# Half of the low weight parts of the first SwiGLU half step: a negated cast and an adding transfer in place of a VectorE subtraction

## The chip, the cores and the metric

The kernel runs on one core of a Trainium2 chip. The metric is the device time of one execution in microseconds; lower is better. Before the change it was 1975.11 us (median of two runs, 1974.4 and 1975.81).

## The reference

One decoder layer on 256 tokens of width 2048, in float32: a SwiGLU half step, a mixer of dilated attention and gated linear attention, cross-attention into 256 memory tokens, and a second SwiGLU half step.

```python
def swiglu(h, w_gate, w_up, w_down):
    return (jax.nn.silu(h @ w_gate) * (h @ w_up)) @ w_down

x = x + 0.5 * swiglu(rms_norm(x, ffn1_norm), ffn1_w_gate, ffn1_w_up, ffn1_w_down)   # D_FF = 5632
x = x + hybrid_mixer(rms_norm(x, mix_norm), pos, w_in, ..., w_out)
x = x + cross_attention(rms_norm(x, xattn_norm), rms_norm(mem, mem_norm), ...)
x = x + 0.5 * swiglu(rms_norm(x, ffn2_norm), ffn2_w_gate, ffn2_w_up, ffn2_w_down)
```

The change concerns the first line of the four alone, and of it only how the weights are prepared.

## The kernel before

**Weights.** All weights are float32 in HBM, packed by the host so that a group of four k tiles (128 rows each) of a chunk of 512 columns is one contiguous megabyte, 8 KB for each of the 128 partitions. TensorE multiplies them as `float32r`, so each weight is split in two parts of that type: `wh`, the weight rounded by a cast on ScalarE (L125), and `wl`, the rest, by a subtraction on VectorE (L126). The tokens (`xT`, `hT`, `mT`) are split the same way into a high and a low part.

**One group.** `wgroup` loads a group into `raw` (L115, issued by SyncE, three buffers) and splits it in two halves of two k tiles each. A half's `wh` and `wl` are tiles of 128 x 1024 elements, 0.5 MB; `WB = 4` buffers each. `mm3` then multiplies one half: for both token tiles and both k tiles three products, tokens' high part by `wh` (L134) and by `wl` (L135), tokens' low part by `wh` (L136), all summed in a PSUM tile `acc`. So a half group is 12 products of 128x128 by 128x512, a group 24.

**Order.** `proj` walks over the groups of a chunk. The loads and the split of the weights stand in `tc.high_priority(WPRI)`, so that they are put ahead in the queues of their engines as far as buffers allow. Products that need other engines' results are put off with `later` by so many half groups.

**The first half step.** `ffn` does eleven chunks of gate and up (four groups each) and then four chunks of down (eleven groups each). The first chunk of gate is split in single k tiles as the tokens arrive (`fine`). `load_x` brings the tokens a second time for their norm; the norm's factor is a power on GpSimd (`rpow`, L214). The second half step uses the same function with other weights.

**GpSimd** has little to do in the first half step: the gains of the tokens' first chunks at the start (L180), the power at 50 us, and memsets for the mixer (L342 and the lines behind it) after it. Before the change GpSimd issues no transfers.

Of the kernel before, what the change touches and what calls it, by code (L numbers as in the profile page):

```python
# [17 lines left out]
S = 256  # L18
# [28 lines left out]
def layer_kernel(ctx: ExitStack, tc: tile.TileContext, A: dict, out: bass.AP):  # L47
# [22 lines left out]

    # products that wait for other engines are put off by so many half groups of a projection
    pend = []
# [13 lines left out]

# [1 line left out]
    gain = con.tile([P, 82], F32, name="gain")  # L88
    # the first loads in the order of their use; what is taken from xload and wload is already under way
    xload, wload = [], []  # L90
# [12 lines left out]

# [1 line left out]
    def wgroup(W, c, g, fine=None):  # L105
        """group g of chunk c of a packed weight, in halves; fine: per k tile, each after fine(k)"""
        n = W.shape[-1]
        kn = W.shape[-2]
        m = kn // 2
        with tc.high_priority(WPRI):  # L110
            if wload:
                raw = wload.pop(0)
            else:
                raw = wp.tile([P, kn, n], F32, tag="raw", name="raw")
                SY.dma_start(raw, W[c, g])  # L115
        for h in range(2):
            with tc.high_priority(WPRI):
                wh = wp.tile([P, m, n], F32R, tag="wh", name="wh", bufs=WB)
                wl = wp.tile([P, m, n], F32R, tag="wl", name="wl", bufs=WB)
                for i in range(m if fine else 1):  # L120
                    d = slice(i, i + 1) if fine else slice(0, m)
                    src = raw[:, m * h + d.start:m * h + d.stop]
                    if fine:
                        fine(m * h + i)
                    SC.copy(wh[:, d], src)  # L125
                    V.tensor_sub(wl[:, d], src, wh[:, d].bitcast(F32))  # L126
            yield [(kn * g + m * h + kk, wh[:, kk], wl[:, kk]) for kk in range(m)]

    def mm3(acc, lhs, half, first, last, ts=range(TT)):
        """adds lhs(k, t).T @ w for the k tiles of a half group"""  # L130
        for t in ts:
            for i, (k, wh, wl) in enumerate(half):
                lh, ll = lhs(k, t)
                PE.matmul(acc[t], lh, wh, start=first and i == 0, stop=False)  # L134
                PE.matmul(acc[t], lh, wl, start=False, stop=False)  # L135
                PE.matmul(acc[t], ll, wh, start=False, stop=last and i == len(half) - 1)  # L136

    def proj(W, c, lhs, groups, fine=None, last=False):
        """sum over the k tiles of the groups of lhs(k, t).T @ W[k, chunk c], for both token tiles"""
        n = W.shape[-1]  # L140
        acc = [pa.tile([P, n], F32, tag="acc", name="acc") for _ in range(TT)]
        groups = list(groups)
        for i, g in enumerate(groups):
            if fine and i:
                fine(4 * i)
            if last and i == len(groups) - 1:
                both = [w for half in wgroup(W, c, g) for w in half]
                for t in range(TT):
                    mm3(acc, lhs, both, i == 0, True, (t,))
                break  # L150
            for h, half in enumerate(wgroup(W, c, g, fine if i == 0 else None)):
                mm3(acc, lhs, half, i == 0 and h == 0, i == len(groups) - 1 and h == 1)
                tick()
        return acc
# [4 lines left out]

# [1 line left out]
    xT = {}  # L161
# [7 lines left out]
    def packed_load(src, k0, n):  # L169
        """n k tiles of a transposed chunk as the host packed it"""  # L170
        xr = U([P, n, S], F32, "xr")
        SY.dma_start(xr, src[k0 // 4, :, k0 % 4:k0 % 4 + n])
        return xr

    def packed(xr, k0, n, hi, lo, g0):
        """gain and split of what packed_load has brought"""
        if n == 1:
            SC.activation(xr[:, 0], xr[:, 0], AF.Copy, scale=gain[:, g0 + k0:g0 + k0 + 1])
        else:
            G.tensor_tensor(xr, xr, gain[:, g0 + k0:g0 + k0 + n].unsqueeze(2).broadcast_to([P, n, S]), op=ALU.mult)  # L180
        SC.copy(hi, xr)
        V.tensor_sub(lo, xr, hi.bitcast(F32))
# [6 lines left out]
    def norm_chunk(c, src, g0, ss):  # L189
        """src [tok, t, 512]: square sums into ss, gained and transposed halves into xT"""  # L190
        sumsq(c, src, ss)

        def turn():
            hi, lo = xtiles(c)
            for t in range(TT):
                tp = PM([P, 4, P], "tp")
                for j in range(4):
                    PE.transpose(tp[:, j], src[:, t, j * P:(j + 1) * P], ident)  # L198
                xg = W2([P, 4, P], "xg")
                V.tensor_tensor(xg, tp, gain[:, g0 + 4 * c:g0 + 4 * c + 4].unsqueeze(2).broadcast_to([P, 4, P]),  # L200
                                op=ALU.mult)
                sl = slice(t * P, (t + 1) * P)
                SC.copy(hi[:, :, sl], xg)
                V.tensor_sub(lo[:, :, sl], xg, hi[:, :, sl].bitcast(F32))

        later(1, turn)
# [20 lines left out]

# [1 line left out]
    def ffn(pre, r, after, fine=None, last=False):  # L229
        wg, wu, wd = (A[f"{pre}_w_{n}"] for n in ("gate", "up", "down"))  # L230
        hT = {}
# [11 lines left out]
        for f in range(NF):  # L243
            acc = proj(wg, f, lhs_x, range(4), fine if f == 0 else None)
            if callable(r):
                r = r()
            sg = []
            for t in range(TT):
                s = W2([P, 512], "sg")
                SC.activation(s, acc[t], AF.Silu, scale=r[:, t:t + 1])  # L250
                sg.append(s)
            acc = proj(wu, f, lhs_x, range(4))
            hs = []
# [9 lines left out]
        for c in range(NC):  # L263
            acc = proj(wd, c, lhs_h, range(NF), last=last and c == NC - 1)
            for t in range(TT):
                V.scalar_tensor_tensor(xs[c][:, t], acc[t], 0.5, xs[c][:, t], op0=ALU.mult, op1=ALU.add)
            after(c)

# [1 line left out]
    def head_scale(acc, r, r2, t, scale_in, sign, name):  # L270
        """per head of 128 columns: sign * r * (r^2 sumsq / 128 + eps)^-1/2, times 128^-1/2 if scale_in"""
        sq = W2([P, 4, HD], "sq")
# [17 lines left out]

# [1 line left out]
    mhalf = con.tile([P, P], F32, name="mhalf")  # L292
    V.memset(mhalf, -0.5)
    # the first function set, and the tensor engine's clock, while the first loads are under way
    warm = ST(1, "warm")
# [31 lines left out]

# [1 line left out]
    win = A["w_in"]  # L329
# [34 lines left out]

    # q, k of the gated heads
    def gated(which, c):
# [20 lines left out]

    # gate ranks, [rank, tok]: 16 columns of w_in, whose two parts are summed by the second product
    r2b = con.tile([P, TT, 32], F32, name="r2b")
# [12 lines left out]

    # log decays: 16 * log_a summed within chunks, [dk, head, tok]
    def decays():
# [30 lines left out]

    # decayed keys back to [tok, dk], the other chunk's rows zero
    kd = []
# [10 lines left out]

    # masked q k^T within chunks, transposed: [j, t, head, i]
    at = per_t("at")  # L450
# [64 lines left out]

    # output norm and gate
    mT = {}
# [26 lines left out]

# [1 line left out]
    # rope tables with the head norms' gains, q's negated  # L546
    gb = W2([P, 4, HD], "gb")
# [110 lines left out]

# [1 line left out]
    ssm = new_ss("ssm")  # L660
# [57 lines left out]

# [1 line left out]
    ss3 = new_ss("ss3")  # L720
# [7 lines left out]

# [1 line left out]
    acc = proj(A["xattn_w_q"], 0, lhs_x, range(4))  # L730
# [71 lines left out]

# [1 line left out]
    def store(c):  # L804
# [8 lines left out]
def _pack(w, n=512):  # L813
    """weights [K, N] as [N / n, groups, 128, k tiles, n]: each group of k tiles is one contiguous megabyte"""
    import numpy as np
# [7 lines left out]
def _columns(x):  # L823
    """tokens [S, D] as [chunks, 128, k tiles, S]"""
    import numpy as np

    return np.ascontiguousarray(np.asarray(x).T.reshape(NC, 4, P, S).transpose(0, 2, 1, 3))
# [26 lines left out]
def _constants():  # L854
    """What depends on the shapes alone: rope angles, which keys a query attends and how often."""
    import numpy as np
# [36 lines left out]
```

## Time and profile before

| | |
|---|---|
| profiled execution, span from the first to the last instruction | 1974.5 us |
| timed runs | 1974.4 and 1975.81 us, median 1975.11 us |
| granted TensorE clock, mean | 0.999 |
| TensorE busy | 1966.5 us |
| VectorE busy | 1039.2 us |
| ScalarE busy | 912.3 us |
| GpSimd busy | 61.2 us |
| read from HBM | 370.72 MB, 189 GB/s over the span |

The profile gives no time of its own for the profiled execution beside the span; the span lies within the timed runs. PE is TensorE's products, PEld its weight loads (they overlap), DVE VectorE, ACT ScalarE, POOL GpSimd, SP SyncE; a q behind a name is that engine's queue of instructions that are not counted as busy. L126 is line 126 of the kernel before. `out<-in` names the tiles an instruction writes and reads. DMA share is the mean busy share of the core's 16 DMA engines. In the timeline a row has the start and duration in us, and in brackets the idle time before it and what ended it.

### The profile page before, as it was taken

The page shows a single profiled execution, that of the slowest core. Times are in us where ns is not written, and L with a number is a line of the kernel's source. Part 1 is how long each engine was busy: PE and PEld are TensorE (multiplying, and loading weights), DVE is VectorE, ACT ScalarE, POOL GpSimd, SP SyncE. Part 2 cuts the span into 40 slices and gives each one's busy share as a digit, 9 for nine tenths or more (in the row PEclk, how much of TensorE's full clock was granted, in tenths as well). Part 3 has the DMA queues.
Part 4 walks back from the last instruction along what each step waited for, and adds up shares of the span by engine and source line. Part 5 has one row for each costly group of instructions (what it writes and reads, how often), then busy time and mean ns, then how long its engine had stood idle before and what let it go on. Part 6 is the DMA issues. An engine that isn't in the chain of part 4 may idle for free.

```text
span 1974.5 us, 22181 instructions
## 1 busy us (share of the span) xinstructions
PE 1966.5 (100%) x9000; PEld 1632.6 (83%) x9000; DVE 1039.2 (53%) x1102; ACT 912.3 (46%) x1115; POOL 61.2 (3%) x61
## 2 busy tenths in 40 slices
PE   9999999999999999999999999999999999999999
PEld 7888888888888888778888889888888888888887
DVE  6455444444455545546785566654444444444443
ACT  6444444444444436444576446544444444433332
POOL 2000000000000000002230000000000000000000
PEclk9999999999999999999999999999999999999999
DMA  8555555555555554445465554455555555555553
GB/s 308 187 191 189 192 192 192 187 188 187 189 190 190 195 204 149 171 156 201 172 219 204 196 186 154 173 192 192 188 187 188 188 189 190 191 192 202 203 204 116
DMA packets 57683, 374.26 MB, mean 190 GB/s; under 512 B 6475, under 2 KB 7627, under 8 KB 13932
## 3 DMA queue, kind: packets, MB, share of 16 engines
q1 hardware_dynamic: 56428, 370.74, 52.2%
q10 hardware_dynamic: 1152, 2.10, 0.3%
q8 instruction: 70, 1.15, 0.2%
q14 instruction: 33, 0.27, 0.0%
HBM read 370.72 MB, written 2.10 MB: 189 GB/s over the span
## 4 chain that ended last, share of the span: by engine, by line
PE 99%; DMA 0%; SPq 0%; DVE 0%; ACT 0%; POOL 0%; issue 0%; POOLq 0%
PE acc L136 32%; PE acc L134 32%; PE acc L135 32%; PE tp L239 1%; PE tp L198 1%; DMA xr<-in_xT_dram 0%; PE dsp L475 0%; PE op L492 0%; PE op L496 0%; PE tp L582 0%; PE sc L595 0%; PE op L629 0%; PE sc L738 0%; PE op L773 0%; PE tp L616 0%; PE zp L409 0%
## 5 line engine op out<-in xcount | busy, mean ns | idle before, releaser
L126 DVE TENSOR_TENSOR wl<-raw,wh 128x1024 fp32r<-128x1024 f32 (+1 forms) x690 | 845.6, 1227 | 855.5 <-ACT wh L125 855.1
L125 ACT CAST wh<-raw 128x1024 fp32r<-128x1024 f32 (+1 forms) x690 | 724.8, 1052 | 965.5 <-PE acc L136 944.6
L134 PE MATMUL acc<-wh,xTh 128*128 128x512 f32 x1824 | 714.8, 392 | 1.8 <-ACT wh L125 1.8
L135 PE MATMUL acc<-wl,xTh 128*128 128x512 f32 x1824 | 710.9, 390 | 1.0 <-DVE wl L126 1.0
L136 PE MATMUL acc<-wh,xTl 128*128 128x512 f32 x1824 | 710.7, 390 | 0.0
L134 PEld LDWEIGHTS acc<-wh,xTh 128*128 128x128 f32 x1824 | 342.5, 188 | 73.6 <-ACT wh L125 3.0
L135 PEld LDWEIGHTS acc<-wl,xTh 128*128 128x128 f32 x1824 | 343.0, 188 | 72.7 <-DVE wl L126 2.5
L136 PEld LDWEIGHTS acc<-wh,xTl 128*128 128x128 f32 x1824 | 342.8, 188 | 71.5
L134 PE MATMUL acc<-wh,hTh 128*128 128x512 f32 x704 | 274.3, 390 | 0.0
L136 PE MATMUL acc<-wh,hTl 128*128 128x512 f32 x704 | 273.9, 389 | 0.0
L135 PE MATMUL acc<-wl,hTh 128*128 128x512 f32 x704 | 273.9, 389 | 0.0
L136 PEld LDWEIGHTS acc<-wh,hTl 128*128 128x128 f32 x704 | 132.1, 188 | 27.5
L134 PEld LDWEIGHTS acc<-wh,hTh 128*128 128x128 f32 x704 | 132.1, 188 | 27.4
L135 PEld LDWEIGHTS acc<-wl,hTh 128*128 128x128 f32 x704 | 132.2, 188 | 27.2
L134 PE MATMUL acc<-wh,mTh 128*128 128x512 f32 x128 | 50.1, 392 | 0.0
L136 PE MATMUL acc<-wh,mTl 128*128 128x512 f32 x128 | 49.8, 389 | 0.0
L135 PE MATMUL acc<-wl,mTh 128*128 128x512 f32 x128 | 49.8, 389 | 0.0
L250 ACT ACTIVATE sg<-acc,r 128x512 f32<-128x512 f32 x44 | 30.1, 687 | 6.1 <-PE acc L136 6.1
L134 PE MATMUL acc<-wh,memh 128*128 128x256 f32 (+1 forms) x96 | 31.4, 327 | 0.0
L256 DVE SCALAR_TENSOR_TENSOR h<-acc,r,sg 128x512 f32<-128x512 f32 x44 | 30.9, 743 | 0.0
L136 PE MATMUL acc<-wh,meml 128*128 128x256 f32 (+1 forms) x96 | 30.6, 318 | 0.0
L135 PE MATMUL acc<-wl,memh 128*128 128x256 f32 (+1 forms) x96 | 30.5, 318 | 0.0
(249 smaller groups left out, 801.3 us busy)
## 6 DMA issues: line engine op xcount, KB each, us to landing
raw<-in_ffn_w_up_dram SPq DMA_DIRECT2D x88, 1024.0 KB, 4.8
raw<-in_ffn_w_down_dram SPq DMA_DIRECT2D x88, 1024.0 KB, 4.8
raw<-in_ffn_w_gate_dram SPq DMA_DIRECT2D x85, 1024.0 KB, 4.8
raw<-in_w_in_dram SPq DMA_DIRECT2D x48, 1024.0 KB, 4.8
raw<-in_w_out_dram SPq DMA_DIRECT2D x16, 1024.0 KB, 4.8
raw<-in_xattn_w_k_dram SPq DMA_DIRECT2D x4, 1024.0 KB, 4.7
raw<-in_xattn_w_q_dram SPq DMA_DIRECT2D x4, 1024.0 KB, 4.7
raw<-in_xattn_w_v_dram SPq DMA_DIRECT2D x4, 1024.0 KB, 4.9
```

Of the source, the lines that this page charges most:

```text
L125: SC.copy(wh[:, d], src)
L126: V.tensor_sub(wl[:, d], src, wh[:, d].bitcast(F32))
L134: PE.matmul(acc[t], lh, wh, start=first and i == 0, stop=False)
L135: PE.matmul(acc[t], lh, wl, start=False, stop=False)
L136: PE.matmul(acc[t], ll, wh, start=False, stop=last and i == len(half) - 1)
L198: PE.transpose(tp[:, j], src[:, t, j * P:(j + 1) * P], ident)
L239: PE.transpose(tp[:, j], hs[t][:, j * P:(j + 1) * P], ident)
L250: SC.activation(s, acc[t], AF.Silu, scale=r[:, t:t + 1])
L256: V.scalar_tensor_tensor(h, acc[t], r[:, t:t + 1], sg[t], op0=ALU.mult, op1=ALU.mult)
```

## The change

For the second half of each group in the first half step (all but the first chunk of gate), `wl` is no longer the difference `raw - wh` made by VectorE. ScalarE casts `raw` a second time with a scale of -1 into `wl`, and a transfer issued by GpSimd then adds the same weights, read again from HBM, onto `wl` in place. The first halves, the first chunk of gate and all other weights are split as before. The rest of the diff takes out comments and docstrings.

```diff
-    def wgroup(W, c, g, fine=None):
+    def wgroup(W, c, g, fine=None, dma=False):
...
         for h in range(2):
             with tc.high_priority(WPRI):
                 wh = wp.tile([P, m, n], F32R, tag="wh", name="wh", bufs=WB)
                 wl = wp.tile([P, m, n], F32R, tag="wl", name="wl", bufs=WB)
+                if dma and h == 1:
+                    SC.copy(wh, raw[:, m:])
+                    SC.activation(wl, raw[:, m:], AF.Copy, scale=-1.0)
+                    G.dma_start(wl, W[c, g][:, m:], accum_op=ALU.add)
+                    yield [(kn * g + m + kk, wh[:, kk], wl[:, kk]) for kk in range(m)]
+                    continue
                 for i in range(m if fine else 1):
...
-    def proj(W, c, lhs, groups, fine=None, last=False):
+    def proj(W, c, lhs, groups, fine=None, last=False, dma=False):
...
-            for h, half in enumerate(wgroup(W, c, g, fine if i == 0 else None)):
+            for h, half in enumerate(wgroup(W, c, g, fine if i == 0 else None, dma)):
...
     def ffn(pre, r, after, fine=None, last=False):
+        dma = pre == "ffn1"
...
-            acc = proj(wg, f, lhs_x, range(4), fine if f == 0 else None)
+            acc = proj(wg, f, lhs_x, range(4), fine if f == 0 else None, dma=dma and f > 0)
...
-            acc = proj(wu, f, lhs_x, range(4))
+            acc = proj(wu, f, lhs_x, range(4), dma=dma)
...
-            acc = proj(wd, c, lhs_h, range(NF), last=last and c == NC - 1)
+            acc = proj(wd, c, lhs_h, range(NF), last=last and c == NC - 1, dma=dma)
```

## The prediction

> **What bounds the kernel now.** I read the page's busy times and its chain first, to see which engine sets the end.
>
> ```profile
> PE 1966.5 (100%) x9000; PEld 1632.6 (83%) x9000; DVE 1039.2 (53%) x1102; ACT 912.3 (46%) x1115; POOL 61.2 (3%) x61
> ...
> PE 99%; DMA 0%; SPq 0%; DVE 0%; ACT 0%; POOL 0%; issue 0%; POOLq 0%
> ```
>
> TensorE is busy for all of the 1974.5 us span, and 99% of the chain lies on it. VectorE, which the change relieves, works half of the time. Whether TensorE ever waits for it is in the chain of waits:
>
> ```profile
> ACT wh L125 <- PE acc L136: 944.6, 603, 3.8
> DVE wl L126 <- ACT wh L125: 855.1, 617, 3.2
> ...
> PEld acc L134 <- ACT wh L125: 3.0, 4, 1.7
> ...
> PEld acc L135 <- DVE wl L126: 2.5, 4, 1.5
> ```
>
> The columns are total us, times and longest. The waits run the other way: ScalarE waits for TensorE to give a weight buffer back, VectorE waits for ScalarE. TensorE's waits for `wl` are 2.5 us in the whole kernel. So there is nothing to gain from a shorter VectorE queue. The question is only whether the new path brings `wl` in time. Two stretches, a settled one of the first half step and the start, show the transfers:
>
> ```profile
> core 0: us, PE busy (x) PEld busy (x) DVE busy (x) ACT busy (x) POOL busy (x), PEclk, DMA share, GB/s
> 10.00:20.00 10.00, 7.68 (x24) 5.30 (x24) 7.76 (x8) 6.10 (x10) 5.76 (x4) 0.83 1.03 407
> ...
> 200.00:400.00 200.00, 200.00 (x900) 165.97 (x899) 98.30 (x89) 86.35 (x91) 0.00 (x0) 1.00 0.53 191
> ```
>
> In the settled stretch TensorE has no idle time at the full clock and the DMA engines are 0.53 busy with 191 GB/s. At the start they are full: 407 GB/s is the most that they moved.
>
> **The budget of one half group.** A half group is two k tiles, twelve products. Its `wh` and `wl` each have four buffers. The timeline shows one turn:
>
> ```profile
> 299.71 0.39 PE L136 MATMUL acc<-wh,xTl 128*128 128x512 f32 x1
> 299.94 0.39 PE L134 MATMUL acc<-wh,xTh 128*128 128x512 f32 x1
> ...
> 300.14 1.05 ACT L125 CAST wh<-raw 128x1024 fp32r<-128x1024 f32 x1 [0.67 <-PE acc L136]
> ...
> 301.23 1.23 DVE L126 TENSOR_TENSOR wl<-raw,wh 128x1024 fp32r<-128x1024 f32 x1 [1.50 <-ACT wh L125]
> ...
> 302.48 11.21 SPq L115 DMA_DIRECT2D raw<-in_ffn_w_gate_dram  x3
> ...
> 302.66 0.39 PE L134 MATMUL acc<-wh,xTh 128*128 128x512 f32 x1
> 302.86 1.05 ACT L125 CAST wh<-raw 128x1024 fp32r<-128x1024 f32 x1 [1.08 <-PE acc L136]
> ...
> 308.10 0.39 PE L134 MATMUL acc<-wh,xTh 128*128 128x512 f32 x1
> ...
> 308.32 0.39 PE L135 MATMUL acc<-wl,xTh 128*128 128x512 f32 x1
> ...
> 313.74 1.05 ACT L125 CAST wh<-raw 128x1024 fp32r<-128x1024 f32 x1 [1.67 <-PE acc L136]
> ```
>
> Half groups start at 299.94 and 302.66, so one takes 2.72 us and a group 5.44 us. The half that ends at 300.10 frees the buffers; the cast into them starts at 300.14. Four buffers mean that they are used again three half groups later, in the half that starts at 308.10, where the first product with `wl` starts at 308.32. Today `wl` is ready at 301.23 + 1.23 = 302.46: 5.9 us to spare.
>
> **The change, part by part.** It concerns the second half of the groups of the first half step: 40 groups of gate (ten column chunks of four), 44 of up, 44 of down, so **128 half groups**.
>
> Removed: 128 subtractions of 1.23 us = 157 us of VectorE. They stand beside a busy TensorE, so they are worth 0. The most that relief of both engines could give is the waits quoted above, under 6 us.
>
> Added on ScalarE: 128 casts of 1.05 us = 135 us. In a settled group it then does 3 x 1.05 = 3.15 of 5.44 us; the 1.67 us of idle time ahead of the last cast shown covers it. But the cast lies on the new path: `wl` holds its negated value only at 300.14 + 2 x 1.05 = 302.24. From there to 308.32 the transfer has **6.1 us**, issue and landing included.
>
> Added on GpSimd: 128 issues, each waiting for the negated cast. Its queue is otherwise nearly empty in this stage:
>
> ```profile
> 49.99 0.72 POOL L214 TENSOR_TENSOR r<-r1m,mhalf 128x2 f32<-128x2 f32 x1 [24.43 <-DVE r1m L220]
> POOL glrT L342 <- PE acc L136: 637.5, 1, 637.5
> ```
>
> Behind a waiting transfer could stand only the one power at 50 us, which the first silu needs, and the memset after the half step. If a transfer stood behind that power instead, it could lose up to 24.4 us, once. I count 0 for it, since the code issues the power's inputs first and the transfers are raised by `WPRI`.
>
> Moved: `raw` was given back when VectorE had read it (302.46, and the load was issued at 302.48). Now it is given back by the negated cast at 302.24, the very moment when the adding transfer is released. **The 1 MB load and the adding transfer of 0.5 MB start together, every group.** The load itself is safe: what was asked for at 302.48 is first needed by the cast at 313.74, three groups on, over 11 us later, against 4.8 us to land (the next row).
>
> ```profile
> 18.39 0.33 SPq L115 DMA_DIRECT2D raw<-in_ffn_w_up_dram  x1
> 18.76 0.43 SPq L320 DMA_DIRECT2D x<-in_x_dram  x1
> ...
> raw<-in_ffn_w_up_dram SPq DMA_DIRECT2D x88, 1024.0 KB, 4.8
> ...
> raw<-in_ffn_w_gate_dram SPq DMA_DIRECT2D x4, 512.0 KB, 8.1
> x<-in_x_dram SPq DMA_DIRECT2D x4, 512.0 KB, 6.8
> ...
> graw<-in_w_rank_dram SPq DMA_DIRECT2D x1, 128.0 KB, 2.7
> ```
>
> The first two rows are issues in the timeline; the others give size and median us from issue to landing. No adding transfer and none issued by GpSimd is in this trace, so its duration D is bounded by these rows. Lower end: a plain 0.5 MB alone, between 2.7 us (128 KB) and 4.8 us (1 MB), on the line between them 3.6 us. Beside another load: `x` is 0.5 MB issued right behind 1 MB of `raw` (18.39 and 18.76), 6.8 us; half a megabyte of `raw` at the crowded start took 8.1 us. Upper end: the sum needs the old content of `wl` as well as the weights, so twice that, 13.6 us.
>
> I take a value nearest to the 1 MB row: two streams of 0.5 MB are read for it, so 4.8 us; the load that starts with it has 1.05 MB to move, which at 407 GB/s is 2.6 us, shared; and GpSimd's power above, on two columns, takes 0.72 us where an issue of SyncE takes 0.33, so I add 0.4 us, an estimate. **D = 7.8 us.** The `x` row with a second stream of 0.52 MB at 407 GB/s gives 6.8 + 1.3 = 8.1, near it.
>
> *The sum.* A `wl` buffer of a second half comes round every four half groups, 10.88 us. If D exceeds 6.1 us the turn is longer by the excess: 128 transfers over the two buffers are 64 turns, and TensorE waits 64 x (7.8 - 6.1) = **109 us**. As a check on bandwidth: the settled 0.53 is one megabyte per group; an adding half counted double makes 1.06 in 5.44 us. Against the 1.03 of the full stretch a group would be 5.60 us, 128 x 0.16 = 20 us, so the turn is the tighter limit, not the bytes. Nothing after the first half step changes. 1974.5 + 109 = **2083 us**. The span of 1974.5 lies inside the shown runs (1974.4 to 1975.81, median 1975.11), so no correction is made. The measurement can tell about 2%, 39.5 us, from no change; that is D = 6.7 us.
>
> The Trainium skill, Collectives: The Full Stack, section The bandwidth ceiling, says that a transfer which adds runs at half the rate of a copy, because it reads two sources through one ring. Nothing in this trace shows it; by that rule the sum would stay at 109 us; without it the plain price, weighed among the rivals, would hold.
>
> **Rivals.**
>
> *The transfer stays hidden* (not slower). If an adding transfer shares so well that it lands within 6.1 us of the cast, TensorE never waits: 1975 us. For it: an ordinary megabyte lands in 4.8 us, the DMA engines are idle almost half of the time. Against: it starts in the load's busiest moment, every time. It decides at D = 6.1 us; up to D = 6.7 us the time stays within 2%, and a transfer that costs no more than a plain one, 3.6 + 2.6 + 0.4 = 6.6 us, falls there too (64 x 0.5 = 32 us, 2007 us). Chance 0.32. The Trainium skill, DMA: Bandwidth & Descriptors, section Anatomy of one DMA, gives a GpSimd-issued transfer 2.0 us plus its bytes at 436 GB/s, an estimate of 3.2 us here, which would make this rival right; no run here shows one yet.
>
> *The transfer is much slower* than the bytes say: the add itself, or GpSimd's writing of 128 row transfers, costs several us each. At the upper end, D = 13.6 us, 64 x 7.5 = 480 us, 2455 us. TensorE would then stand still for several us at a time, and the 10-20 us row shows a granted clock of 0.83 where it was 7.68 of 10 us busy: a further loss. For it: nothing in the trace bounds the price of the add. Chance of D over 10.4 us: 0.16.
>
> *VectorE was the hidden limit* (faster). It would need products waiting for `wl`; the waits are under 6 us in all, 0.3%. Chance of over 2%: 0.01.
>
> **How the numbers follow.** The forecast, D between 6.7 and 10.4 us (2013 to 2250 us), has 0.51. Within 2% is 0.32, slower by over 2% 0.51 + 0.16 = 0.67, faster 0.01. The range takes in the hidden case and the forecast's whole, 1972 to 2250 us, and leaves out the slow tail.
>
> **What the profile would show.** If I am right: the memset behind the first half step, which runs at 49.99 + 0.72 + 637.5 = 688 us, comes near 795; before it TensorE's idle time ahead of the products with `wl` is released by DMA, about 1.7 us each second group or 0.85 each; the new transfers land in 7 to 9 us, the loads of `raw` in over 4.8; the DMA share there is about 0.8 to 0.9, and 128 x 0.52 = 67 MB more come from HBM; from the mixer on all is as before. If the transfer is hidden, the settled stretch has TensorE at 200 of 200 us with D under 6.1. What would make me wrong: a D far from 7.8, up or down, since every us of it is 64 us of time; or a TensorE clock below 1.00 in the waits.

## The result and the profile after

The changed kernel takes 2208.75 us (two runs, 2206.84 and 2210.66) against 1975.11 us: a ratio of 1.1184, 95% interval [1.1166, 1.1202]. It is slower, as forecast, and the time lies within the range of 1972 to 2250 us. But the forecast was 109 us more and the measured change is 234 us, over twice as much.

The page of the changed kernel, busy times, chain by engine, and transfers by queue (packets, MB, share of 16 engines' span):

```profile
PE 2033.0 (92%) x9000; PEld 1650.9 (75%) x9000; DVE 884.8 (40%) x974; ACT 1032.8 (47%) x1243; POOL 172.0 (8%) x189
...
q0 software_dynamic: 18432, 67.12, 18.9%
...
PE 67%; DMA 24%; issue 6%; ACT 2%; DVE 0%; SPq 0%; POOL 0%; POOLq 0%; ACTq 0%
...
wl<-in_ffn_w_up_dram POOLq DMA_DIRECT2D x44, 512.0 KB, 8.7
wl<-in_ffn_w_down_dram POOLq DMA_DIRECT2D x44, 512.0 KB, 8.5
wl<-in_ffn_w_gate_dram POOLq DMA_DIRECT2D x40, 512.0 KB, 8.3
```

VectorE lost 154 us of work, ScalarE gained 120, and neither matters. A quarter of the chain is now the adding transfers, which land in 8.3 to 8.7 us. TensorE still makes 9000 products, but is busy 66.5 us longer. What it waits for, in the chain of waits:

```profile
PE acc L142 <- DMA wl<-in_ffn_w_up_dram: 57.9, 34, 4.0
...
PE acc L142 <- DMA wl<-in_ffn_w_down_dram: 54.6, 33, 2.8
...
PE acc L142 <- DMA wl<-in_ffn_w_gate_dram: 43.0, 28, 2.6
...
PE acc L141 <- ACT sg L258: 8.9, 1, 8.9
```

The first three are 155.5 us. With 66.5 us of longer work that is 222 of the 230.6 us by which the span grew (2205.1 against 1974.5). The last row is the rest: one wait for the first silu, which needs the power on GpSimd, and that ran at 71.79 us instead of 49.99. All of it lies in the first half step: from the end of that step's last product to the end of the span it is 1232.0 us in both kernels. Two stretches of that step:

```profile
core 0: us, PE busy (x) PEld busy (x) DVE busy (x) ACT busy (x) POOL busy (x), PEclk, DMA share, GB/s
60.00:690.00 630.00, 519.84 (x2150) 406.09 (x2149) 134.61 (x132) 288.79 (x310) 75.75 (x87) 0.96 0.83 216
200.00:400.00 200.00, 166.44 (x678) 129.84 (x677) 41.40 (x40) 91.29 (x97) 23.55 (x27) 0.95 0.83 216
```

The DMA engines are at 0.83, not full, and the granted clock is below 1.00. One turn in the timeline:

```profile
300.82 0.87 POOL L124 DMA_DIRECT2D wl<-in_ffn_w_gate_dram  x1 [10.80 <-ACT wl L123]
...
301.49 0.33 SPq L116 DMA_DIRECT2D raw<-in_ffn_w_gate_dram  x1
...
306.26 0.87 POOL L124 DMA_DIRECT2D wl<-in_ffn_w_gate_dram  x1 [4.57 <-ACT wl L123]
306.29 0.39 PE L141 MATMUL acc<-wh,xTh 128*128 128x512 f32 x1
...
309.15 0.79 PE L142 MATMUL acc<-wl,xTh 128*128 128x512 f32 x1 [2.47 <-DMA wl<-in_ffn_w_gate_dram]
309.75 0.63 PE L143 MATMUL acc<-wh,xTl 128*128 128x512 f32 x1
310.17 0.63 PE L141 MATMUL acc<-wh,xTh 128*128 128x512 f32 x1
...
312.81 0.40 PE L142 MATMUL acc<-wl,xTh 128*128 128x512 f32 x1
313.04 0.40 PE L143 MATMUL acc<-wh,xTl 128*128 128x512 f32 x1
...
313.47 1.05 ACT L132 CAST wh<-raw 128x1024 fp32r<-128x1024 f32 x1 [6.57 <-PE acc L143]
...
314.63 1.06 ACT L123 ACTIVATE wl<-raw 128x1024 fp32r<-128x1024 f32 x1
...
315.98 0.87 POOL L124 DMA_DIRECT2D wl<-in_ffn_w_gate_dram  x1 [8.85 <-DMA wl<-in_ffn_w_gate_dram]
```

A transfer issued at 300.82 lets TensorE go on at 309.15. The products behind the wait start 0.42 us apart (309.75, 310.17) and only later 0.23 us (312.81, 313.04): they run at half clock for a while. At 313.47 a cast of a *first* half gets its buffer back, at 314.63 the negated cast, and at 315.98 the next transfer goes into that turn.

That first half's buffer comes back in the middle of things, and this is what the code does not show. TensorE's queue, as the program was built, for one group of each kernel (runs of products, by half and token tile t):

```
before:  first half t0 x6, first half t1 x6, second half t0 x6, second half t1 x6
after:   first half t0 x6, second half t0 x6, first half t1 x6, second half t1 x6
```

The change never touches the products, but the planner that fills the queues put them in another order. The trace bears it out: of the 24 weight loads of a group, those that wait for a new part are the 1st, 2nd, 13th and 14th in the kernel before, and the 1st, 2nd, 7th and 8th in the changed one.

### The profile page after: what moved, and what is told of

Read it like the earlier page. It is cut to its first block, busy times and chain, and to the rows that moved or that the text cites. A ratio compares the mean times of both kernels' runs of the same rounds, so it can differ in the third digit from the quotient of the medians.

```text
span 2205.1 us, 22581 instructions
## 1 busy us (share of the span) xinstructions
PE 2033.0 (92%) x9000; PEld 1650.9 (75%) x9000; DVE 884.8 (40%) x974; ACT 1032.8 (47%) x1243; POOL 172.0 (8%) x189
## 4 chain that ended last, share of the span: by engine, by line
PE 67%; DMA 24%; issue 6%; ACT 2%; DVE 0%; SPq 0%; POOL 0%; POOLq 0%; ACTq 0%
PE acc L142 22%; PE acc L143 21%; PE acc L141 21%; DMA wl<-in_ffn_w_up_dram 8%; DMA wl<-in_ffn_w_down_dram 8%; DMA wl<-in_ffn_w_gate_dram 7%; ACT wl L123 2%; PE tp L247 0%; PE tp L205 0%; DMA xr<-in_xT_dram 0%; PE dsp L483 0%; PE op L500 0%; PE op L504 0%; PE tp L590 0%; PE sc L603 0%
## 5 line engine op out<-in xcount | busy, mean ns | idle before, releaser
L133 DVE TENSOR_TENSOR wl<-raw,wh 128x1024 fp32r<-128x1024 f32 (+1 forms) x562 | 689.4, 1228 | 1187.1 <-ACT wh L132 1186.6
L132 ACT CAST wh<-raw 128x1024 fp32r<-128x1024 f32 (+1 forms) x562 | 589.6, 1051 | 1035.6 <-PE acc L143 987.8
L142 PE MATMUL acc<-wl,xTh 128*128 128x512 f32 x1824 | 729.1, 400 | 102.0 <-DMA wl<-in_ffn_w_up_dram 57.9
L141 PE MATMUL acc<-wh,xTh 128*128 128x512 f32 x1824 | 724.1, 397 | 10.3 <-ACT sg L258 8.9
L142 PE MATMUL acc<-wl,hTh 128*128 128x512 f32 x704 | 283.3, 402 | 54.6 <-DMA wl<-in_ffn_w_down_dram 54.6
L123 ACT ACTIVATE wl<-raw 128x1024 fp32r<-128x1024 f32 x128 | 136.2, 1064 | 12.9 <-PE acc L142 4.1
L122 ACT CAST wh<-raw 128x1024 fp32r<-128x1024 f32 x128 | 132.0, 1031 | 1.7 <-PE acc L143 1.5
L124 POOL DMA_DIRECT2D wl<-in_ffn_w_down_dram x44 | 38.4, 873 | 281.2 <-ACT wl L123 254.3
L124 POOL DMA_DIRECT2D wl<-in_ffn_w_up_dram x44 | 38.5, 876 | 275.4 <-ACT wl L123 275.4
L124 POOL DMA_DIRECT2D wl<-in_ffn_w_gate_dram x40 | 34.9, 873 | 261.7 <-ACT wl L123 238.8
```

Of the source, the lines that this page charges most:

```text
L122: SC.copy(wh, raw[:, m:])
L123: SC.activation(wl, raw[:, m:], AF.Copy, scale=-1.0)
L124: G.dma_start(wl, W[c, g][:, m:], accum_op=ALU.add)
```

## The experiments

Theory A: the buffer's turn (last use, cast, issue, landing, first use) is too long, in part because of TensorE's new order. Theory B: the adding transfers fill the DMA engines. Theory C: starting together with the load of `raw` makes them slow. A further question is what the lower clock costs. The edits are shown shortened, with comments that are not in the code.

**Three buffers for the transferred parts.**

```diff
-                wh = wp.tile([P, m, n], F32R, tag="wh", name="wh", bufs=WB)
-                wl = wp.tile([P, m, n], F32R, tag="wl", name="wl", bufs=WB)
+                wh = wp.tile([P, m, n], F32R, tag="wh", name="wh", bufs=3)
+                wl = wp.tile([P, m, n], F32R, tag=f"wl{h}", name="wl", bufs=2 + h)
```

> Same work, but the low parts of the second halves get three buffers of their own (first halves two, high parts three instead of four; the same memory). A buffer then comes round every six half groups, 16.3 us. If the wait for the way round (cast, issue, 8.4 us to landing, use) was the cause, it is hidden: 5 x 2.72 = 13.6 us against about 1.1 + 1.1 + 0.3 + 8.4 = 10.9 us, and the time is 1975 to 1990 us at a clock of 1.00. If the transfers' bytes are the limit (in the first half step of the changed kernel the loads' packets were busy 2.83 us and the adding transfers' 3.25 us per group, 6.08 us), a group takes at least 6.08/1.03 = 5.90 us and the time is at least 1974.5 + 128 x 0.46 = 2033 us.

Measured: 2039.97 us, ratio 1.0339 [1.0319, 1.0358]. Theories A and B both hold, one after the other: 169 us were the turn, and what is left, 65 us, is the limit by bytes that the expectation put at 2033 us or more. The stretch of this kernel:

```profile
200.00:400.00 200.00, 192.74 (x850) 155.14 (x849) 52.44 (x52) 109.96 (x118) 29.69 (x34) 1.00 0.97 267
```

The DMA engines are full at 0.97 and the clock is back at 1.00. What is late now is the load of `raw`, in the waits from 200 to 600 us:

```profile
ACT wl L123 <- DMA raw<-in_ffn_w_gate_dram: 71.8, 27, 4.6
ACT wl L123 <- DMA raw<-in_ffn_w_up_dram: 56.1, 27, 4.5
ACT wl L123 <- DMA raw<-in_ffn_w_down_dram: 25.9, 12, 3.6
```

**The first half added instead of the second.**

```diff
-                if dma and h == 1:
+                if dma and h == 0:          # and the slices raw[:, :m], W[c, g][:, :m]
```

> The adding transfer makes the low part of the first half of a group instead of the second, so that it no longer starts in the moment in which the load buffer is given back. If starting together with the 1 MB load makes the landing 8.4 us, it falls by up to 2.6 us to about 6, and the time to 1980 to 2060 us. If the adding transfer is slow by itself, landing stays near 8.4 us and the time near 2205 us.

Measured: 2207.99 us (ratio 1.1179 [1.1156, 1.1201]), no different from the change. The issues from 200 to 600 us:

```profile
raw<-in_ffn_w_up_dram SPq DMA_DIRECT2D x28, 1024.0 KB, 5.7
raw<-in_ffn_w_gate_dram SPq DMA_DIRECT2D x28, 1024.0 KB, 5.6
wl<-in_ffn_w_gate_dram POOLq DMA_DIRECT2D x28, 512.0 KB, 8.1
wl<-in_ffn_w_up_dram POOLq DMA_DIRECT2D x28, 512.0 KB, 8.0
```

For comparison the changed kernel in the same stretch, and the landing of all its adding transfers:

```profile
raw<-in_ffn_w_gate_dram SPq DMA_DIRECT2D x28, 1024.0 KB, 8.0
raw<-in_ffn_w_up_dram SPq DMA_DIRECT2D x27, 1024.0 KB, 8.1
wl<-in_ffn_w_up_dram POOLq DMA_DIRECT2D x28, 512.0 KB, 8.7
wl<-in_ffn_w_gate_dram POOLq DMA_DIRECT2D x27, 512.0 KB, 8.3
```

```profile
DMA to landing us min/median/max: 7.2/8.4/10.4
```

The load gains, 5.6 to 5.7 instead of 8.0 us; the adding transfer hardly does, 8.0 to 8.1 instead of 8.3 to 8.7. But the edit did not take the two apart, as its timeline shows:

```profile
315.79 0.33 SPq L116 DMA_DIRECT2D raw<-in_ffn_w_up_dram  x1
315.94 0.88 POOL L124 DMA_DIRECT2D wl<-in_ffn_w_gate_dram  x1 [5.52 <-ACT wl L123]
```

In the changed kernel the load starts 0.67 us behind the transfer (300.82 and 301.49), here 0.15 us ahead of it. Of the 128 transfers of this run 96 start within 0.2 us of a load and land in 8.4 us (median); 26 start 1.4 to 2.3 us behind one and land in 7.2. So theory C was not tested by this run. Those 26 speak for a part of it, about 1.2 us, but they are not spread evenly (in the stretch above, most are every fourth transfer), so that is not shown either.

**The products with the low part last.**

```diff
+        if late:      # second halves: both products with wh for every k tile and t, then all with wl
...
```

> In the second halves the eight products with the high part of the weights go first and the four with the low part last. The first use comes 1.6 us later and the buffer is given back 0.2 us later. If the way round is the cause, each of the 64 turns loses about 1.4 us of wait (90 us) and the gaps become too short to lower the clock (67 us): about 2050 us. If the DMA engines are the limit, or the clock falls for another reason, nothing changes: about 2200 us.

Measured: 2205.44 us (1.1166 [1.1144, 1.1188]): the expectation of 2050 us failed. Its timeline says why:

```profile
309.34 0.88 POOL L124 DMA_DIRECT2D wl<-in_ffn_w_gate_dram  x1 [6.43 <-ACT wl L123]
310.60 0.73 PE L146 MATMUL acc<-wl,xTh 128*128 128x512 f32 x2 [0.93 <-DMA wl<-in_ffn_w_gate_dram]
311.17 0.40 PE L152 MATMUL acc<-wh,xTh 128*128 128x512 f32 x1
...
312.75 1.06 ACT L132 CAST wh<-raw 128x1024 fp32r<-128x1024 f32 x1 [3.69 <-PE acc L154]
...
313.71 1.05 ACT L122 CAST wh<-raw 128x1024 fp32r<-128x1024 f32 x1
...
314.66 1.05 ACT L123 ACTIVATE wl<-raw 128x1024 fp32r<-128x1024 f32 x1
...
316.01 0.88 POOL L124 DMA_DIRECT2D wl<-in_ffn_w_gate_dram  x1 [5.79 <-ACT wl L123]
```

After two products with `wl` (L146) comes the first half's other token tile (L152): the queue is interleaved here too, so the first use came only three products later, not seven. And ScalarE's queue now has the negated cast (L123) last of three casts, 1 us later. So this run tested the turn with an edit that did not shorten it, and says nothing against theory A.

**Zero products in the gaps.**

```diff
+                for _ in range(fill if i == 0 and t == 0 else 0):      # fill = 4 in the second halves
+                    PE.matmul(acc[t], zero, wh, start=False, stop=False)
```

> Four more products per second half, with a left side of zeros, stand ahead of its first product with the low part: 128 x 4 x 0.227 = 116 us more work for TensorE, which leaves the result as it is. If 67 of the 234 us are lost to a granted clock that falls after gaps of 2.5 us and more, the products fill the gaps, the clock is near 1.00 and the time falls, to 2140 to 2170 us. If the clock costs nothing by itself, the time stays at 2205 us or rises by up to 116 us.

Measured: 2181.66 us (1.1045 [1.1023, 1.1068]). TensorE does 116 us more and the kernel is 27 us faster than with the change alone. The direction is as expected, the size is not. The stretch:

```profile
200.00:400.00 200.00, 186.80 (x813) 148.94 (x812) 42.40 (x40) 93.55 (x98) 24.50 (x28) 1.00 0.88 221
```

The clock is 1.00 instead of 0.95. But TensorE is busy 2114.6 us in this run, 32 us more than 1966.5 + 116, at a mean clock of 0.996: only about half of the 66.5 us is the clock. Most of the rest stays at a nearly full clock; the next run shows where.

**TensorE's order undone.**

```diff
-                PE.matmul(acc[t], lh, wh, start=first and i == 0, stop=False)
+                one = PE.matmul(acc[t], lh, wh, start=first and i == 0, stop=False)
+                if pin and i == 0:      # in the first half step: not ahead of what stands before it in the code
+                    tc.keep_in_program_order(one)
```

> The changed kernel with one thing undone: in its queue TensorE takes six products of the first half, six of the second, then six and six again for the other token tile; here the first product of each half and token tile is pinned behind what stands before it, so that the order is twelve and twelve, as in the kernel before. The first product with the transferred low part is then the 14th of the group instead of the 8th, 1.36 us later, while the buffer comes free at the same place. If the order took that from the budget, each of the 64 turns waits 1.4 us instead of 2.5 us, the gaps lower the clock less, and the time is 2060 to 2100 us. If the order is of no consequence, 2205 us.

Measured: 2107.01 us, ratio 1.0664 [1.0648, 1.068]. The order alone is worth 102 us. Busy times and waits:

```profile
PE 2000.7 (95%) x9000; PEld 1628.2 (77%) x9000; DVE 885.8 (42%) x974; ACT 1031.0 (49%) x1243; POOL 171.6 (8%) x189
```

```profile
PE acc L144 <- DMA wl<-in_ffn_w_up_dram: 34.7, 31, 4.1
...
PE acc L144 <- DMA wl<-in_ffn_w_down_dram: 27.8, 31, 2.0
PE acc L144 <- DMA wl<-in_ffn_w_gate_dram: 21.0, 22, 1.7
```

The waits fall from 155.5 to 83.5 us. TensorE's busy time is still 34 us over that of before, at a mean clock of 0.996. One of its products behind a wait:

```profile
309.00 0.50 PE L144 MATMUL acc<-wl,xTh 128*128 128x512 f32 x1 [1.61 <-DMA wl<-in_ffn_w_up_dram]
```

It lasts 0.50 us where 0.39 is usual, 0.11 more, and the product ahead of it has nothing behind it to overlap with: usually the next one starts after 0.23 us, so 0.16 us of its 0.39 count as busy that otherwise would not. So each wait costs more than its idle time, by an estimate 0.27 us, or 23 us for the 84 waits shown.

**The order alone, without the transfer.** The kernel before with its products pinned in the changed kernel's order.

```diff
+            if inter:      # the first half step
+                halves = list(wgroup(W, c, g))
+                for t in range(TT):
+                    for h, half in enumerate(halves):
+                        mm3(acc, lhs, half, ..., (t,), pin=True)
```

> The kernel before, with no transfer added, but with TensorE's products of the first half step pinned in the order of the changed kernel (six of the first half, six of the second, then six and six for the other token tile). If that order costs only by what it takes from the budget of a slow low part, it costs nothing here, where the low part is ready 2.3 us after its buffer comes free: 1974 to 1980 us. If the order itself slows TensorE, the time is above 2000 us.

Measured: 1976.01 us, ratio 1.0004 [0.9995, 1.0013]. The order costs nothing where the low part is early.

**Three buffers and the order of before.** The first edit and the one that undoes the order, together.

> Three buffers of its own for the transferred low part and the products pinned in the order of before, twelve and twelve. If the DMA engines are the only limit left with three buffers, the order changes nothing: 2033 to 2045 us and a DMA share of 0.97. If the order still cost something there, the time falls below 2020 us.

Measured: 2036.36 us, ratio 1.0317 [1.0299, 1.0335], with a DMA share of 0.97 from 200 to 400 us. With three buffers the order is not what counts.

**A plain transfer.**

```diff
-                    G.dma_start(wl, W[c, g][:, m:], accum_op=ALU.add)
+                    G.dma_start(wl, W[c, g][:, m:])
```

> The transfer from GpSimd writes the weights over the low part instead of adding them (the low part is then the weight itself: the sum is left out). If the add, with its second stream, is what makes the landing 8.4 us, it falls to 5.8 to 7 us, the packets' busy time from 3.25 us per transfer to about 1.5, and the time to 2000 to 2110 us. If GpSimd's issue and the way through its queue make it, the landing stays above 8 us and the time near 2205 us.

This kernel leaves the sum out. Measured: 2115.43 us (1.071 [1.0675, 1.0744]), a little over what was expected. The whole kernel's landing times and, from 200 to 600 us, its queue from GpSimd; behind them the same queue of the run with the order undone, which keeps the add:

```profile
DMA to landing us min/median/max: 4.2/5.9/8.9
```

```profile
q0 software_dynamic: 8827, 32.15, 31.7%
```

```profile
q0 software_dynamic: 8960, 32.64, 50.7%
```

Same bytes, 61 and 62 transfers in 400 us: 2.07 us of the 16 engines' time for one plain transfer (0.317 x 400 / 61.3), 3.26 for an adding one (0.507 x 400 / 62.3). Without the add the median landing is 5.9 us instead of 8.4. But this median stands between two groups: 63 of the 128 transfers land within 5.2 us and 57 take 7.5 us or more, where with the add 127 of 128 do. So the kernel still waits 79 us for transfers, at 35 products. Why a plain transfer is sometimes as slow as an adding one, no run here tells.

**Half of the bytes added.**

```diff
-                    SC.activation(wl, raw[:, m:], AF.Copy, scale=-1.0)
-                    G.dma_start(wl, W[c, g][:, m:], accum_op=ALU.add)
+                    SC.activation(wl[:, 1:], raw[:, m + 1:], AF.Copy, scale=-1.0)
+                    G.dma_start(wl[:, 1:], W[c, g][:, m + 1:], accum_op=ALU.add)
+                    V.tensor_sub(wl[:, 0:1], raw[:, m:m + 1], wh[:, 0:1].bitcast(F32))
```

> Only one of the two k tiles of the second half is added by the transfer, 256 KB; VectorE subtracts the other. If the landing goes with the bytes, it falls to 5 to 6 us, under what the buffer's turn leaves, and the time to 1975 to 2000 us. If it is mostly a fixed price per transfer, it stays above 7.5 us and the time above 2120 us.

Measured: 2020.25 us (1.0228 [1.0207, 1.0248]), slower than expected, between the two cases and far nearer to the first. The landing falls with the bytes:

```profile
DMA to landing us min/median/max: 4.3/5.7/9.4
```

5.7 us for 256 KB and 8.4 for 512 KB: on a straight line through these two medians, an estimate, 2.7 us for each 256 KB and about 3 us for what does not depend on them.

**Three buffers and a plain transfer.** The first edit and the plain transfer's, together.

> Three buffers of its own for the transferred low part, and the transfer writes over instead of adding (the sum is left out). If the remaining 65 us of the kernel with three buffers are the adding transfers' bytes, which count more than twice on the DMA engines, the DMA share falls from 0.97 to about 0.8 and the time to 1975 to 1985 us. If they come from the order or from GpSimd, the time stays at 2040 us.

This kernel leaves the sum out too. Measured: 1985.08 us, ratio 1.0048 [1.0031, 1.0065], at the upper end of what was expected. The stretch:

```profile
200.00:400.00 200.00, 200.00 (x901) 165.95 (x900) 55.77 (x54) 120.90 (x128) 19.36 (x36) 1.00 0.84 284
```

TensorE has no gap, with more bytes per second (284 against 267) and a lower DMA share (0.84 against 0.97). The queue from GpSimd from 200 to 600 us, with three buffers and the add, and without it:

```profile
q0 software_dynamic: 9735, 35.49, 50.5%
```

```profile
q0 software_dynamic: 10278, 37.42, 29.4%
```

That is 2.98 us of the engines for an adding transfer (0.505 x 400 / 67.7) and 1.65 for a plain one (0.294 x 400 / 71.4). So 55 of the last 65 us are the price of the add on the DMA engines, and not that of reading the weights twice, with which about 10 us remain. No version with the adding transfer can gain on the kernel before, since TensorE is already busy throughout there; none was faster.

## Why the prediction was right or wrong

**What bounds the kernel, and the sign: right.** VectorE's 154 us were worth nothing, and the end is set by a buffer's turn in the first half step. From the mixer on nothing changed.

**The landing, D: mis-sized by 0.9 us.** I took 7.8 us from the end of the cast. Measured are 8.4 us from the issue, and the issue starts 0.3 us after the cast. In the sum that makes 2141 us; that the measured time still lies within the range is due to its width, since what brought it to 2209 us is not in the sum. In the chip's price for the add I was near: half a megabyte that is added takes 3.26 us of the engines against 2.07 plain, 1.6 times; with three buffers it is 2.98 against 1.65 us, 1.8 times. The Trainium skill, Collectives: The Full Stack, section The bandwidth ceiling, says twice, of the adding step of a collective; the second pair comes nearer to that. The Trainium skill, DMA: Bandwidth & Descriptors, section Anatomy of one DMA, gives 2.0 us plus bytes at 436 GB/s, by an estimate 3.2 us here, which would have hidden the transfer. Even the fastest plain one of these runs took 3.9 us, beside the loads.

**My reason for D stays open.** I put 2.6 of its 7.8 us down to the load that starts together with it. The run with the first half added was to part the two and did not: the two still start 0.15 us apart. Which of them goes first changed the load's landing by 2.4 us and the transfer's by about 0.4. The few transfers that started later behind a load landed 1.2 us sooner.

**The budget of 6.1 us: the step that failed.** It was read off the timeline of before, with TensorE's order taken as given. The changed program has another order; the first product that needs the transferred part is the 8th of the group, not the 14th: 1.36 us less in each turn. I also had the two casts of the second half in the wrong order: the negated one comes first, which gives back 1.05 us. With the order undone the kernel takes 2107 us, 131 us more than before, where the sum said 109. That this is near is partly luck, since errors cancel in it: D was 0.9 us too short (58 us in 64 turns), the budget 1.05 us too short by the order of the casts (67 us the other way), and of the 128 us by which the span of that run grew only 83.5 are waits for transfers; 34 are longer work. The planner's order is the other 102 us.

**The rate of 64 us for each us of D: fits the order, not the plain transfer.** The order's 1.36 us should make 87 us of waits; the waits moved by 155.5 - 83.5 = 72 us, and TensorE's longer work behind them by 32. Without the add the median landing fell by 2.5 us, which should save 160 us; 93 were saved. Nearly half of those transfers land hardly sooner, and one number for D hides that.

**What stops TensorE costs more than the stop.** The sum counted idle time alone; 66.5 us of longer products came on top. About half is the granted clock: by the trace's records of it products were busy for 80 us at half speed, 3 us in the kernel before, and half of the difference, 38 us, is lost. It nearly goes away with the gaps filled or shortened. Of the 34 us in the run with the order undone, by the same records about 5 are the clock and 23, by the estimate above, what the 84 waits cost beside their idle time. I had named the clock as a risk for waits of several us only; waits of 2.5 us were enough. The Trainium skill, TensorE: Matmul & The Clock Gate, section What's actually happening, gives an idle window of about 3.4 us before the clock is halved; the 2.47 us row above was followed by half speed, so here less was enough. The 20 stretches at half speed between 60 and 950 us say more: in the 3.4 us ahead of each, TensorE had stood idle for 1.8 to 2.6 us in all. The same time has 30 waits of over 2 us, so not every one of them is followed by half speed.

**The power on GpSimd: 9 us where I counted 0.** My reason held, since no transfer held it up: what ended its queue's idle time was its input from VectorE. But that input came later, as the fourth load of the tokens was issued at 61.10 us instead of 36.34, and TensorE waited 8.95 us for the silu, once.

**The bandwidth check of 20 us: too low.** With the turn out of the way the bytes cost 61 to 65 us. The 1.06 was near. The 1.03 was not: I took it from the start, and with three buffers the DMA engines stood at 0.97. With that, 1.06 in 5.44 us becomes 5.94 us a group, 64 us in all. An added half megabyte cost 2.98 to 3.26 us of the engines, near the 2.9 us (0.53 x 5.44) of one loaded megabyte, as which I had counted it.

**The signs named in advance.** The memset behind the half step came at 902.9 us, not near 795 (807.8 with the order undone). The waits by DMA ahead of the products with `wl` are there. The DMA share, 0.83, and the 67 MB are as said. The landing of 8.3 to 8.7 us is inside "7 to 9".

## What to carry to other kernels

Before a slack that is read from the old timeline is used as a budget for a slower operand, look at the queues of the changed program: the planner may order even untouched instructions anew and eat part of the slack. Moving work from an idle engine into transfers pays only if the buffers cover the whole turn, and the turn has the landing beside real traffic in it. By these runs a transfer that adds should be priced as at least one and a half plain ones, and each wait of the busiest engine somewhat above its idle time. An edit that is to move a transfer, or to lengthen a slack, has to be looked up in the new timeline as well: two of these experiments did not do what they were meant to.

## What the runs showed of the hardware

An adding transfer of 0.5 MB, weights from HBM added onto a tile on the core, lands in 8.4 us (median) beside loads of 1 MB per group. The same without the add lands in 4.2 to 8.9 us, about half of them within 5.2 us, and 256 KB with it in 5.7 us (median). In DMA engine time the adding transfer costs 1.6 to 1.8 times the plain one. Two transfers that start within 0.7 us of each other: which goes first changed the landing of the load of 1 MB by 2.4 us, that of the adding one by about 0.4. TensorE fell to half speed after an idle time of 2.47 us, and 20 times in the changed kernel after 1.8 to 2.6 us of idle time within 3.4 us. Four products with zeros in each of the 128 half groups made the kernel 27 us faster.
